# Columns of a matmul taken in pieces: five orders of the moving operand and the PSUM bank in a feed-forward

## The chip, the cores and the metric

The kernel runs on one core of one Trainium2 chip. The metric is the device time of one execution in microseconds (us). Times of whole kernels are medians over runs; the profile comes from one execution of its own.

## The reference

A trunk of two decoder layers over 1024 positions of width 1024, all in float32. Layer 0 mixes by a gated linear recurrence beside attention to a memory of 256 positions; layer 1 mixes by attention in a sliding window of 128 beside memory attention. Each mixer is followed by a gated feed-forward of inner width 2816. The change touches the first half of the feed-forward of layer 0:

```
def swiglu_ffn(x, w_in, w_out):
    gu = x @ w_in
    g, u = gu[..., :D_FF], gu[..., D_FF:]
    return (jax.nn.silu(g) * u) @ w_out
...
f = swiglu_ffn(rms_norm(h, norm_ffn_pre[l]), w_ffn_in[l], w_ffn_out[l])
h = h + rms_norm(f, norm_ffn_post[l])
```

## The kernel before

Activations are kept transposed: 128 features on the partitions, 512 positions along the columns of a tile, so 1024 x 1024 activations are 8 x 2 tiles. To get float32 accuracy from a cheaper matmul format (float32r), each operand is split into a high part, rounded to that format (ScalarE, L95), and the rest (VectorE, L96). A product then takes three matmuls for each 128 features: high weight by low activation (L700), high by high (L701), low by high (L702). All add up in one PSUM bank of 128 x 512 float32. Each matmul reads its 512-column moving operand from SBUF and writes the whole bank; its weights, 128 x 128, are loaded by LDWEIGHTS (in the profile: engine PEld) while the matmul before it still runs.

The inner width of 2816 is 22 blocks of 128. Blocks 0 and 1 are made plainly (`ffn_plain`). Blocks 2 to 21 are made by `gated`: gate and up half of the weights, two halves of the 1024 features and two halves of the positions are treated as 2 x 2 matrices, whose product takes seven block products instead of eight, with sums and differences of weights (GpSimd, L720 to L725) and of activations made beforehand. Each of the seven is one call of `product`: four groups of 128 features, three matmuls each, so 12 matmuls, and 84 for a gated block. The seven add into three banks of tag `mm` (there are seven of them in rotation). `copy`, `gate`, `mul` and `add` read a bank when a product has ended, on ScalarE (L730, L734) and VectorE (L711, L715).

The kernel is written with a framework whose scheduler sets the order of instructions on each engine from priorities (`high_priority`) and its own simulation of time, and which adds the waits between engines. Weights arrive by DMA in the tiles `wq` and `wp`, are split into `ch` and `cl`; activations stand in `ah`/`al` and, for the sums and differences, in `th`/`tl`.

After the blocks, `out_product` (L808 to L810) makes the second half of the feed-forward, and layer 1 follows, with a feed-forward of its own that goes through the same functions with `layer` equal to 1.

Of the kernel before, what the change touches and what calls it, by code (L numbers as in the profile page):

```python
# [43 lines left out]
POST_STEPS = range(4, 20, 2)  # L44
LATE_PRODUCTS, LAST_STEPS = (2, 5, 3), range(36, 132, 12)
OUT_PARTS = {1: (0, 0), 2: (1, 0), 3: (1, 0), 4: (1, 1), 5: (1, 1), 6: (0, 0), 7: (0, 1)}
CLOSE_POOL = (4, "th21"), (5, "tl21")
NO_SYNC = mybir.DependencyInfo(mybir.DependencyClass.NoSync, mybir.DependencyReason.DATA)
SHUF = list(range(8, 16)) + list(range(0, 8)) + list(range(16, 32))
# [2 lines left out]
class Trunk:  # L52
# [639 lines left out]
                hid.append(hu)  # L692
        return hid, mms

    def product(self, out, w, x, start=True):
        mm, ins = self.nc.tensor.matmul, []
        for k in range(4):
            wh, wl = (v[:, k] for v in w)
            xh, xl = x[k]
            ins += [mm(out, wh, xl, start=start and k == 0, stop=False, skip_group_check=not start),  # L700
                    mm(out, wh, xh, start=False, stop=False, skip_group_check=not start),  # L701
                    mm(out, wl, xh, start=False, stop=k == 3, skip_group_check=not start)]  # L702
        return ins

    def gated(self, layer, b, xs, order=(1, 5, 6, 2, 7, 3, 4), ring="wq", eng=None, lead=WEIGHT_LEAD):
        nc = self.nc
        eng = eng or nc.gpsimd
        with self.tc.high_priority(offset=WEIGHT_LEAD):
            a11, a12, a21, a22 = self.quads(ring, *(self.a["wi"][layer, u * NFB + b] for u in range(2)))
        made, sums, hid, part = {}, {}, {}, {}  # L710
        add = lambda o, x, y: nc.vector.tensor_tensor(o, x, y, op=ALU.add)  # L711

        def mul(i, x, y):
            hid[i] = self.t("hd")
            return nc.vector.tensor_tensor(hid[i], x, y, op=ALU.mult)  # L715

        def source(i):
            if i in (5, 6) and 5 not in made:
                made[5] = self.t("x", (P, 4, P))
                eng.tensor_tensor(made[5], a21, a22, op=ALU.add)  # L720
                eng.tensor_tensor(a21, a11, a21, op=ALU.subtract)
            if i == 6:
                eng.tensor_tensor(a11, made[5], a11, op=ALU.subtract)
            if i == 3:
                eng.tensor_tensor(a12, a12, a11, op=ALU.subtract)  # L725
            return {1: a11, 2: a12, 3: a12, 4: a22, 5: made.get(5), 6: a11, 7: a21}[i]

        def copy(i, ps):
            part[i] = self.t({1: "c1", 5: "c7", 6: "c6"}[i])
            return nc.scalar.copy(part[i], ps)  # L730

        def gate(i, ps):
            add(part[i], part[i], ps)
            return nc.scalar.activation(part[i], part[i], AF.Silu)  # L734

        steps = {1: (0, lambda ps: copy(1, ps)),
                 5: (1, lambda ps: copy(5, ps)),
                 6: (0, lambda ps: copy(6, ps)),
                 2: (2, lambda ps: gate(1, ps)),
                 7: (0, lambda ps: add(part[5], part[5], ps)),  # L740
                 3: (1, lambda ps: (gate(6, ps), mul(1, part[6], part[5]))),
                 4: (0, lambda ps: mul(0, part[1], ps))}
        for i in order:
            with self.tc.high_priority(offset=WEIGHT_LEAD if i in (1, 2) else lead):
                src = source(i)
                w = self.t("ch", (P, 4, P), F32R), self.t("cl", (P, 4, P), F32R)
                self.split(*w, src)
            c, evict = steps[i]
            chained = c in sums
            ps = sums.setdefault(c, None if chained else self.psum("mm"))  # L750
            mms = self.product(ps, w, xs[i], start=not chained)
            with self.tc.high_priority(offset=EVICT_LEAD):
                ins = evict(ps)
                if i == 7:
                    self.evicted = ins
            yield mms
        self.hid = hid[0], hid[1]
# [34 lines left out]
    def out_operands(self, layer, i, p, xs, ws):  # L792
        nc = self.nc
        block, half = OUT_PARTS[i]
        src = self.wz[p, block] if i in (3, 5, 6, 7) else self.a["wf"][layer, 2 * p + block]
# [45 lines left out]
    def ffn(self, layer, x, act, hx, finish, dst, final):  # L841
# [133 lines left out]
        for i, cs in enumerate(chunks):  # L975
# [14 lines left out]
            rsc.append(self.rstd([s22[:, cs]] + qs, f"m{i}", "c1", cs.stop - cs.start, copy=i == 0)[1])  # L990
        scaled = {k: self.t(tag)[:, :H // 2] for k, tag in CLOSE_POOL}
        for k, x in scaled.items():
# [402 lines left out]
```

## Time and profile before

| | |
|---|---|
| median of 3 runs | 1966.38 us (1965.18 to 1969.33) |
| profiled execution, whole | 1966.28 us |
| profiled execution, span from first to last instruction | 1964.1 us |
| granted TensorE clock, mean over the span | 0.996 of full speed |
| TensorE matmul (PE), busy | 1937.3 us, 9382 instructions |
| TensorE weight load (PEld), busy | 1629.2 us |
| VectorE (DVE), busy | 1399.5 us |
| ScalarE (ACT), busy | 1017.2 us |
| GpSimd (POOL), busy | 429.1 us |
| DMA, mean | 184 GB/s |

Line numbers are those of the kernel before; in the changed kernel, lines behind the new helper stand five further down (L700 to L702 are L705 to L707). In rows such as `mm<-al,ch 128*128 128x512` the written tile stands before the arrow, then the moving operand and the weights, then the shapes. A busy time of matmuls counts the union of rows that overlap, since one matmul begins before the one ahead of it has left the array.

### The profile page before, as it was taken

The page shows a single profiled execution, that of the slowest core. Times are in us where ns is not written, and L with a number is a line of the kernel's source. Part 1 is how long each engine was busy: PE and PEld are TensorE (multiplying, and loading weights), DVE is VectorE, ACT ScalarE, POOL GpSimd, SP SyncE. Part 2 cuts the span into 40 slices and gives each one's busy share as a digit, 9 for nine tenths or more (in the row PEclk, how much of TensorE's full clock was granted, in tenths as well). Part 3 has the DMA queues.
Part 4 walks back from the last instruction along what each step waited for, and adds up shares of the span by engine and source line. Part 5 has one row for each costly group of instructions (what it writes and reads, how often), then busy time and mean ns, then how long its engine had stood idle before and what let it go on. Part 6 is the DMA issues. An engine that isn't in the chain of part 4 may idle for free.

```text
span 1964.1 us, 27864 instructions
## 1 busy us (share of the span) xinstructions
PE 1937.3 (99%) x9382; PEld 1629.2 (83%) x9382; DVE 1399.5 (71%) x2315; ACT 1017.2 (52%) x1942; POOL 429.1 (22%) x439
## 2 busy tenths in 40 slices
PE   9999999999999999999999999999999999999997
PEld 8887888788888888888788888887888888888887
DVE  8888977976767676455786898669656665754566
ACT  6677974534444444454554778554333333344551
POOL 0122110034443320000035454100223232300001
PEclk9999999999999999999999999999999999999999
DMA  5522436167768789775563333361645444585663
GB/s 185 171 86 81 158 119 227 66 231 256 239 242 279 255 287 326 238 233 174 201 213 141 115 112 108 103 262 39 213 134 168 161 156 153 201 301 194 214 197 129
DMA packets 184686, 361.71 MB, mean 184 GB/s; under 512 B 20448, under 2 KB 26336, under 8 KB 184544
## 3 DMA queue, kind: packets, MB, share of 16 engines
q1 hardware_dynamic: 183824, 359.29, 53.6%
q8 instruction: 73, 1.20, 0.2%
q10 hardware_dynamic: 720, 0.66, 0.1%
q14 instruction: 69, 0.57, 0.1%
HBM read 251.86 MB, written 105.91 MB: 182 GB/s over the span
## 4 chain that ended last, share of the span: by engine, by line
PE 87%; DVE 6%; ACT 3%; issue 2%; DMA 1%; POOL 1%; SPq 0%; DVEq 0%; ACTq 0%; POOLq 0%
PE mm L700 12%; PE mm L702 12%; PE mm L701 12%; PE mm L808 7%; PE mm L809 7%; PE mm L810 7%; PE mm L164 6%; PE mm L165 6%; PE mm L166 6%; PE oo L1210 1%; PE tt L1203 1%; PE mm L680 1%; PE mm L679 1%; PE oo L249 1%; PE mm L681 1%
## 5 line engine op out<-in xcount | busy, mean ns | idle before, releaser
L95 ACT CAST ch<-wq 128x512 fp32r<-128x512 f32 x311 | 193.6, 623 | 419.0 <-PE mm L701 212.1
L96 DVE TENSOR_TENSOR cl<-wq,ch 128x512 fp32r<-128x512 f32 x311 | 237.1, 763 | 186.9 <-ACT ch L95 115.8
L700 PE MATMUL mm<-al,ch 128*128 128x512 f32 x640 | 249.6, 390 | 2.9 <-ACT c L730 2.9
L701 PE MATMUL mm<-ah,ch 128*128 128x512 f32 x640 | 249.2, 389 | 0.0
L702 PE MATMUL mm<-ah,cl 128*128 128x512 f32 x640 | 249.0, 389 | 0.0
L164 PE MATMUL mm<-al,wh 128*128 128x512 f32 x552 | 218.1, 395 | 0.6 <-ACT wh L95 0.6
L165 PE MATMUL mm<-ah,wh 128*128 128x512 f32 x552 | 217.1, 393 | 0.0
L166 PE MATMUL mm<-ah,wl 128*128 128x512 f32 x552 | 216.9, 393 | 0.0
L808 PE MATMUL mm<-tl,ch 128*128 128x512 f32 x532 | 207.4, 390 | 0.6 <-ACT ah L910 0.3
L809 PE MATMUL mm<-th,ch 128*128 128x512 f32 x532 | 207.0, 389 | 0.0
L810 PE MATMUL mm<-th,cl 128*128 128x512 f32 x532 | 206.3, 389 | 0.0
L700 PE MATMUL mm<-tl,ch 128*128 128x512 f32 x480 | 187.4, 390 | 0.2
L701 PE MATMUL mm<-th,ch 128*128 128x512 f32 x480 | 186.8, 389 | 0.0
L702 PE MATMUL mm<-th,cl 128*128 128x512 f32 x480 | 186.6, 389 | 0.2 <-DVE cl L96 0.2
L711 DVE TENSOR_TENSOR c<-c,mm 128x512 f32<-128x512 f32 x120 | 82.4, 686 | 98.6 <-PE mm L702 98.3
L700 PEld LDWEIGHTS mm<-al,ch 128*128 128x128 f32 x640 | 120.2, 188 | 28.3 <-ACT c L730 3.7
L702 PEld LDWEIGHTS mm<-ah,cl 128*128 128x128 f32 x640 | 120.2, 188 | 25.0
L701 PEld LDWEIGHTS mm<-ah,ch 128*128 128x128 f32 x640 | 120.2, 188 | 24.7
L720 POOL TENSOR_TENSOR x<-wq,wq 128x512 f32<-128x512 f32 x36 | 53.8, 1494 | 320.0 <-DMA wq<-in_wi_dram 311.8
L166 PEld LDWEIGHTS mm<-ah,wl 128*128 128x128 f32 x552 | 103.9, 188 | 21.9 <-DVE wl L96 0.7
L164 PEld LDWEIGHTS mm<-al,wh 128*128 128x128 f32 x552 | 103.9, 188 | 21.2 <-ACT wh L95 1.0
L165 PEld LDWEIGHTS mm<-ah,wh 128*128 128x128 f32 x552 | 104.0, 188 | 20.2
(424 smaller groups left out, 4324.8 us busy)
## 6 DMA issues: line engine op xcount, KB each, us to landing
wq<-in_wi_dram SPq DMA_DIRECT2D x168, 256.0 KB, 4.6
xz<-hd SPq DMA_DIRECT2D x154, 256.0 KB, 4.2
th<-xz SPq DMA_DIRECT2D x154, 256.0 KB, 3.5
wp<-in_wf_dram SPq DMA_DIRECT2D x112, 256.0 KB, 4.2
wz<-wp SPq DMA_DIRECT2D x88, 256.0 KB, 2.3
wq<-wz SPq DMA_DIRECT2D x56, 256.0 KB, 3.5
wraw<-in_wa_dram SPq DMA_DIRECT2D x26, 512.0 KB, 3.5
wq<-in_wf_dram SPq DMA_DIRECT2D x42, 256.0 KB, 3.9
```

The source lines that it names most:

```text
L95: self.cast = self.nc.scalar.copy(hi, src)
L96: return (eng or self.nc.vector).tensor_tensor(lo, src, hi.bitcast(F32), op=ALU.subtract)
L164: self.mms += [nc.tensor.matmul(out, wh, al, start=i == 0, stop=False), nc.tensor.matmul(out, wh, ah, start=False, stop=False), nc.tensor. ...
L165: nc.tensor.matmul(out, wh, ah, start=False, stop=False),
L166: nc.tensor.matmul(out, wl, ah, start=False, stop=i == len(ks) - 1)]
L700: ins += [mm(out, wh, xl, start=start and k == 0, stop=False, skip_group_check=not start), mm(out, wh, xh, start=False, stop=False, skip_g ...
L701: mm(out, wh, xh, start=False, stop=False, skip_group_check=not start),
L702: mm(out, wl, xh, start=False, stop=k == 3, skip_group_check=not start)]
L711: add = lambda o, x, y: nc.vector.tensor_tensor(o, x, y, op=ALU.add)
L808: ins += [mm(ps[m], wh[:, m], xl[:, cs], start=start and p == 0, stop=False, skip_group_check=not start), mm(ps[m], wh[:, m], xh[:, cs], s ...
L809: mm(ps[m], wh[:, m], xh[:, cs], start=False, stop=False, skip_group_check=not start),
L810: mm(ps[m], wl[:, m], xh[:, cs], start=False, stop=p == NFB // 2 - 1, skip_group_check=not start)]
```

## The change

`product` gets a further argument `g`, two numbers (b, d). If it is given, the 512 columns are taken as `a` groups of `b` pieces of `d` columns, and the matmul goes through them with the piece number outermost: first piece 0 of every group, then piece 1 of every group, and so on. The PSUM bank and both parts of the moving operand are viewed alike, so each column of the product still lands at its own place in the bank. With (2, 2), for instance, a matmul takes columns 0, 1, 4, 5, 8, 9, ... and then 2, 3, 6, 7, ...; with (2, 128) it takes 0 to 127, 256 to 383, 128 to 255, 384 to 511. Gated blocks from 4 on in layer 0 take their pair from the tuple `WOVEN` by the block's number modulo 6; the first entry is None, so blocks 6, 12 and 18 stay as they were.

```
+WOVEN = None, (2, 2), (2, 8), (2, 16), (8, 16), (2, 128)
...
-    def product(self, out, w, x, start=True):
+    def woven(self, x, g):
+        return x if g is None else x.rearrange("p (a b d) -> p b a d", b=g[0], d=g[1])
+
+    def product(self, out, w, x, start=True, g=None):
         mm, ins = self.nc.tensor.matmul, []
+        out = self.woven(out, g)
         for k in range(4):
             wh, wl = (v[:, k] for v in w)
-            xh, xl = x[k]
+            xh, xl = (self.woven(v, g) for v in x[k])
             ins += [mm(out, wh, xl, start=start and k == 0, stop=False, skip_group_check=not start),
...
-            mms = self.product(ps, w, xs[i], start=not chained)
+            mms = self.product(ps, w, xs[i], not chained, WOVEN[b % 6] if layer == 0 and b > 3 else None)
```

| pattern (b, d) | blocks | pieces in a matmul | shape printed below |
|---|---|---|---|
| none | 6, 12, 18 | 1 | 128x512 |
| (2, 2) | 7, 13, 19 | 256 pieces of 2 | 128x2x128x2 |
| (2, 8) | 8, 14, 20 | 64 pieces of 8 | 128x2x32x8 |
| (2, 16) | 9, 15, 21 | 32 pieces of 16 | 128x2x16x16 |
| (8, 16) | 4, 10, 16 | 32 pieces of 16 | 128x8x4x16 |
| (2, 128) | 5, 11, 17 | 4 pieces of 128 | 128x2x2x128 |

The order of instructions on TensorE, with the semaphores that each waits for, at the place where block 6 ends and block 7 begins (the bank mm_4518 is block 6's, mm_4696 is block 7's first). Before:

```order
L701 MATMUL mm_4518<-th_708_3374,ch_4593 128x512
L702 MATMUL mm_4518<-th_708_3374,cl_4594 128x512
L700 MATMUL mm_4696<-al_3125,ch_4692 128x512 [waits Activation_49]
L701 MATMUL mm_4696<-ah_3124,ch_4692 128x512
L702 MATMUL mm_4696<-ah_3124,cl_4693 128x512 [waits DVE_49]
L700 MATMUL mm_4696<-al_3130,ch_4692 128x512
```

and now:

```order
L706 MATMUL mm_4518<-th_708_3374,ch_4593 128x512
L707 MATMUL mm_4518<-th_708_3374,cl_4594 128x512
L705 MATMUL mm_4696<-al_3125,ch_4692 128x2x128x2 [waits Activation_49]
L706 MATMUL mm_4696<-ah_3124,ch_4692 128x2x128x2
L707 MATMUL mm_4696<-ah_3124,cl_4693 128x2x128x2 [waits DVE_49]
L705 MATMUL mm_4696<-al_3130,ch_4692 128x2x128x2
```

Nothing moved; the shape in which the bank is written is another. So it is at every place of the program: the rows of TensorE differ in 1260 shapes, 252 of each pattern, and those of VectorE, ScalarE, GpSimd and the DMA queue don't differ.

Ten first matmuls of a bank get a wait on TensorE's own count, and one matmul loses such a wait (the first sum over partitions behind the feed-forward). The first of the ten is in block 16, on the same engine. Before:

```order
L701 MATMUL mm_6305<-th_791_3833,ch_6343 128x512
L702 MATMUL mm_6305<-th_791_3833,cl_6344 128x512
L700 MATMUL mm_6365<-al_3145,ch_6361 128x512
L701 MATMUL mm_6365<-ah_3144,ch_6361 128x512
L702 MATMUL mm_6365<-ah_3144,cl_6362 128x512 [waits DVE_49]
```

and now:

```order
L706 MATMUL mm_6305<-th_791_3833,ch_6343 128x8x4x16
L707 MATMUL mm_6305<-th_791_3833,cl_6344 128x8x4x16
L705 MATMUL mm_6365<-al_3145,ch_6361 128x8x4x16 [waits PE_49]
L706 MATMUL mm_6365<-ah_3144,ch_6361 128x8x4x16
L707 MATMUL mm_6365<-ah_3144,cl_6362 128x8x4x16 [waits DVE_49]
```

The matmul that it waits for, the last into the bank before, stands some 180 rows ahead of it; for the nearest of the ten it is some 90 rows.

## The prediction

> **What bounds the kernel now.** I read the page's shares first, then the chain, then the stage that the change touches, and last the single matmuls.
>
> ```profile
> span 1964.1 us, 27864 instructions
> PE 1937.3 (99%) x9382; PEld 1629.2 (83%) x9382; DVE 1399.5 (71%) x2315; ACT 1017.2 (52%) x1942; POOL 429.1 (22%) x439
> PE   9999999999999999999999999999999999999997
> ...
> PE 87%; DVE 6%; ACT 3%; issue 2%; DMA 1%; POOL 1%; SPq 0%; DVEq 0%; ACTq 0%; POOLq 0%
> ```
>
> TensorE is busy for 1937.3 of 1964.1 us, in every slice but the last, and 87% of the chain that ended last is its matmuls. The page also warns that a busy PE need not be PE at its peak, so the stage has to be looked at by itself. The blocks that the change touches run from about 406.5 to 756.0 us. The columns of the next rows are the stretch, its length, busy time with number of instructions of PE, PEld, DVE, ACT and POOL, the granted clock, the DMA share and GB/s.
>
> ```profile
> 406.50:756.00 349.50, 349.31 (x1541) 288.93 (x1540) 251.79 (x346) 150.05 (x262) 134.28 (x94) 1.00 0.76 263
> 478.32:497.36 19.04, 19.04 (x85) 15.77 (x85) 11.19 (x16) 7.92 (x14) 8.87 (x6) 1.00 0.68 232
> ...
> 744.88:763.92 19.04, 19.04 (x85) 15.77 (x85) 12.06 (x20) 9.62 (x17) 0.00 (x0) 1.00 0.95 327
> ```
>
> TensorE is idle for 0.2 of 349.5 us, at a granted clock of 1.00, while VectorE and ScalarE have a quarter to a half of each block free. One block is 7 products of 12 matmuls, 84 in all, and takes 19.04 us, so a matmul takes 19.04/84 = 226.7 ns from start to start. The single rows agree:
>
> ```profile
> 468.41 0.39 PE L700 MATMUL mm<-tl,ch 128*128 128x512 f32 x1
> 468.63 0.39 PE L701 MATMUL mm<-th,ch 128*128 128x512 f32 x1
> 468.86 0.39 PE L702 MATMUL mm<-th,cl 128*128 128x512 f32 x1
> 469.09 0.39 PE L700 MATMUL mm<-tl,ch 128*128 128x512 f32 x1
> ```
>
> Each lasts 0.39 us but the next starts 0.227 us after it: they overlap. The price of a matmul is the 226.7 ns between starts, not the 0.39 us of its row. Whatever a matmul of this stage gains or loses in start-to-start time goes straight to the end of the kernel, because nothing else sets the pace here, nor afterwards:
>
> ```profile
> PE mm L702 <- DVE cl L96: 0.2, 1, 0.2
> ...
> 756.00:1000.00 244.00, 242.90 (x1102) 201.31 (x1102) 148.97 (x244) 120.78 (x220) 10.24 (x9) 1.00 0.65 219
> 1000.00:1300.00 300.00, 295.14 (x1759) 260.00 (x1758) 238.46 (x552) 195.84 (x509) 113.70 (x162) 0.99 0.44 155
> 1300.00:1660.00 360.00, 357.85 (x1595) 295.52 (x1594) 242.89 (x350) 141.70 (x241) 87.75 (x61) 1.00 0.43 146
> 1660.00:1930.00 270.00, 270.00 (x1255) 226.21 (x1254) 167.20 (x253) 127.17 (x226) 24.12 (x17) 1.00 0.62 207
> ```
>
> The first row is the only wait of TensorE in 406 to 756 us (us in total, times, longest). The others show 1.1, 4.9, 2.2 and 0.0 us of idle TensorE in the four later stretches: there is no later slack in which a loss could vanish.
>
> **The change, part by part.** It adds no instruction and removes none; the order on VectorE, ScalarE, GpSimd and the DMA queue is the same row for row. What changes is the order in which 15 of the 18 blocks take the 512 columns: 15 x 84 = 1260 matmuls, 252 in each of the five patterns (blocks 6, 12 and 18 stay plain). Moving operand and PSUM bank are permuted alike, so the same columns meet and the readers of the bank find them where they were. LDWEIGHTS reads the same 128 contiguous columns as before.
>
> The term that decides is 1260 times the difference in start-to-start time of a plain and a woven matmul. No plain matmul of this kernel reads its moving operand or writes its bank in pieces, so the trace has no row for it, and I bound it from both sides.
>
> From below: what a matmul spends beyond its columns. Ten matmuls of 256 columns stand between these first two rows, and the third has eight of 128 columns in another format:
>
> ```profile
> 996.69 0.28 PE L1257 MATMUL mm<-wh,al 128*128 128x256 f32 x1
> ...
> 997.88 1.05 PE L261 MATMUL oo<-ident,rcp 128*128 128x128 f32 x8
> ...
> L261 PE MATMUL oo<-ident,rcp x56: 270/275/275, 284.1 to 1905.5; 128*128 128x128 f32 x56
> ```
>
> (997.88 - 996.69)/10 = 119.0 ns for 256 columns. So a column costs (226.7 - 119.0)/256 = 0.421 ns, and a matmul has 226.7 - 512 x 0.421 = 11.3 ns besides its columns. A new order of the columns can't make fewer of them; if it saved all of the 11.3 ns, 1260 matmuls would give 14.2 us, the end below. That part is alike at 256 and at 512 columns, so it belongs to the instruction and not to the order, and I expect nothing of it.
>
> From above: the slowest columns that the trace has. The eight of L261 are plain fp32, not the split format of the products; (1.05 - 0.275)/7 = 110.7 ns for 128 columns, against 0.06 us here for a matmul of 128 columns in the split format:
>
> ```profile
> 1080.16 0.22 PE L1179 MATMUL ss<-kl,qs 128*128 128x128 f32 x1
> 1080.22 0.28 PE L1180 MATMUL ss<-kh,qs 128*128 128x128 f32 x1
> ```
>
> Columns at about half the rate therefore exist on this engine: 4 x 110.7 = 443 ns for 512, 216 ns over the plain price. If all five patterns ran so, 1260 x 216 ns = 272 us; if only one did, 252 x 216 ns = 54.5 us.
>
> Between the ends I take the value of the rows nearest to "in pieces", although they are of ScalarE and of LDWEIGHTS. L377 writes its 256 columns as four runs of 64 with gaps of 64, L359 the same 256 without gaps; L261's weights are one column read 128 times, L700's lie side by side (the source view: ns min/median/max):
>
> ```profile
> L359 ACT ACTIVATE gi<-mm,rcm 128x256 f32<-128x256 f32 x4 | 1.9, 473 | 4.2 <-POOL rcm L254 4.1
> L377 ACT ACTIVATE vv<-mm,rcn 128x256 fp32r<-128x256 f32 x4 | 1.9, 473 | 3.5 <-PE mm L1259 3.5
> ...
> L261 PEld LDWEIGHTS oo<-ident,rcp x56: 187/190/192, 283.9 to 1905.4; 128*128 128x128 f32 x56
> L700 PEld LDWEIGHTS mm<-al,ch x640: 186/188/192, 328.9 to 1739.5; 128*128 128x128 f32 x160
> ```
>
> 473 against 473 ns, and 190 against 188: a pattern with steps costs nothing there. Both are slower per column than a matmul (473/256 = 1.8 ns against 0.421), so they say little of the finest pieces, and that is where I leave room.
>
> [...]
>
> Beside the patterns, the new program makes ten first matmuls of a bank wait on TensorE's own count, and drops one such wait. In the order the bank's former matmuls lie a block or more back, 19 us, so the wait is over when it is reached: 0. If each instead let the matmul before it drain, it would cost 389 - 227 = 162 ns, ten of them 1.6 us (389 is the median of the row below, min/median/max).
>
> ```profile
> L700 PE MATMUL mm<-al,ch x640: 389/389/499, 328.9 to 1739.7; 128*128 128x512 f32 x160
> ```
>
> Sum: 0 + 0. The profiled execution took 1966.28 us (span 1964.1), 0.1 below the median of the three runs; I give the median, 1966.4.
>
> **Rivals.**
> 1. *Pieces of two columns are too fine.* In pattern (2, 2) a pass takes two columns and skips two, so wherever the operand's memory or the bank serves four neighbours or more at once, half of what is fetched or opened is left for the second pass. It decides as soon as that service is the slower side. Then the 252 matmuls of blocks 7, 13 and 19 run at half rate: 54.5 us by the row above, 252 x 226.7 ns = 57.1 us if the whole matmul doubles. That gives 2020.8 to 2023.4. For it: a block has no idle microsecond to hide it. Against it: pieces of 8 and more, four of the five patterns, would be served whole, and nothing in the trace shows such a limit.
>    [...]
> 2. *Each break costs a column's time.* Pieces per matmul are 256, 64, 32, 32 and 4, together 388; 388 x 0.421 ns x 252 = 41.2 us, 2007.5. For it: a break needs a new address. Against it: three gaps on L377 cost under 1 ns together.
> 3. *All five patterns run at half rate*, because any step in the pattern makes the bank open each column by itself: 1966.3 + 272 = 2239. Against it: pieces of 128 columns have three breaks in 512. [...]
> 4. *Faster*, by the 11.3 ns of a matmul, down to 1952. Only if that gap came from neighbouring columns meeting in the bank; its being alike at two sizes speaks against it.
>
> **How the numbers follow.** A change of 0.2%, 3.9 us, is about what a measurement of this kernel can tell from none; it is 3.1 ns on each woven matmul, or 15.6 ns if only (2, 2) pays. No cost: 0.57. Rival one 0.27, two 0.06, three 0.07, faster 0.03. So slower 0.27 + 0.06 + 0.07 = 0.40, same 0.57, faster 0.03. The likeliest case alone would lie in 1962 to 1971 (0.2% either way, with the 1.6 us of the waits). With rival one the range has to reach 2024, and then holds 0.57 + 0.27 + 0.06 = 0.90; left out are rival three and a gain.
>
> **What would show it.** In the profile after, 406 to 756 us should keep blocks of 19.04 us, with L705 to L707 at 389 ns in every shape. Rival one shows as blocks of some 37 us from about 463, 578 and 692 us on (later ones shifted by what was lost), at busy TensorE and otherwise unchanged waits; rival two as blocks of graded length, rival three as 15 long blocks with three short ones among them. A loss with all blocks at 19.04 us would mean that I missed a wait. The prediction is wrong, too, if the clock in the stage falls below 1.00.

## The result, and the profile after

The changed kernel takes 2029.1 us (median of 4 runs, 2027.18 to 2030.15) where the kernel before takes 1966.1 (4 runs on the same chip, 1965.18 to 1969.33): a ratio of 1.0316, with a 95% interval of 1.0298 to 1.0334. It is slower by 63 us, in the direction and nearly by the amount of rival one, and above the top of the range.

The page of the changed kernel, its span and busy row, then the shares of the chain that ended last:

```profile
span 2027.8 us, 27863 instructions
PE 1999.1 (99%) x9382; PEld 1632.8 (81%) x9382; DVE 1396.3 (69%) x2315; ACT 1017.4 (50%) x1942; POOL 425.7 (21%) x439
PE 88%; DVE 6%; ACT 2%; issue 2%; DMA 1%; POOL 0%; SPq 0%; DVEq 0%; ACTq 0%; POOLq 0%
```

TensorE is busy for 61.8 us more with the same 9382 matmuls; the other engines are busy as long as they were, to within 4 us. Nothing else became the bound. The stretches of the first half of the feed-forward, from its first gated matmul to the first matmul of the second half (L700 to L808 before, L705 to L813 now), before and after (stretch, length, busy time with instructions of PE, PEld, DVE, ACT and POOL, clock, DMA share, GB/s):

```profile
328.95:756.05 427.10, 424.77 (x1885) 350.36 (x1884) 313.82 (x447) 184.74 (x320) 139.31 (x98) 1.00 0.66 227
```

```profile
330.25:820.72 490.47, 487.92 (x1884) 355.58 (x1884) 311.10 (x447) 185.96 (x320) 137.21 (x98) 1.00 0.58 200
```

The stage is 63.4 us longer, TensorE's idle time in it is 2.3 us before and 2.6 after, and the clock stays at 1.00. So the whole loss is matmuls that take longer, in this stage, and the span (+63.7) shows that nothing of it was won back later. The single matmuls say which ones. First where block 7, pattern (2, 2), begins behind a plain bank, then inside it, then inside block 9, pattern (2, 16) (start, duration):

```profile
471.99 0.39 PE L706 MATMUL mm<-th,ch 128*128 128x512 f32 x1
472.22 0.39 PE L707 MATMUL mm<-th,cl 128*128 128x512 f32 x1
472.45 0.61 PE L705 MATMUL mm<-al,ch 128*128 128x512 f32 x1
...
479.68 0.64 PE L706 MATMUL mm<-th,ch 128*128 128x512 f32 x1
480.13 0.63 PE L707 MATMUL mm<-th,cl 128*128 128x512 f32 x1
480.59 0.63 PE L705 MATMUL mm<-tl,ch 128*128 128x512 f32 x1
...
532.86 0.40 PE L705 MATMUL mm<-tl,ch 128*128 128x512 f32 x1
533.09 0.41 PE L706 MATMUL mm<-th,ch 128*128 128x512 f32 x1
533.34 0.40 PE L707 MATMUL mm<-th,cl 128*128 128x512 f32 x1
```

A (2, 2) matmul starts 0.45 us after the one ahead of it; its own duration rises from 0.39 to 0.63 us. A (2, 16) matmul shows almost nothing in its duration, 0.40, but its neighbours start 0.23 and 0.25 us apart. Again the start-to-start time is the price. Its mean over the 84 matmuls of a block, from all single rows of the stage, is the same to 0.2 ns in the three blocks of each pattern (neighbouring blocks interleave by some products, so a block's matmuls are counted by their banks). For (2, 2) the table has the price in an unbroken row inside the block; the mean of all 84 is 452.3 ns, which makes 56.9 us. The plain 226.7 ns are those of the kernel before; the plain blocks 12 and 18 stand at 227.2 here.

| pattern | pieces | ns from start to start | more than plain, ns | x 252 matmuls, us |
|---|---|---|---|---|
| none | 1 | 226.7 | | |
| (2, 2) | 256 of 2 | 453.3 in an unbroken row | 226.6 | 57.1 |
| (2, 8) | 64 of 8 | 232.9 | 6.2 | 1.6 |
| (2, 16) | 32 of 16 | 239.8 | 13.1 | 3.3 |
| (8, 16) | 32 of 16 | 231.7 | 5.0 | 1.3 |
| (2, 128) | 4 of 128 | 227.4 | 0.7 | 0.2 |

The sum is 63.5 us, or 63.3 with the mean of all 84, against 63.4 measured in the stage. Pattern (2, 2) takes twice the plain time and makes 90% of the loss. The last column is not in the order of the number of pieces.

### The profile page after: what moved, and what is told of

It reads as the page before. It is cut to its first block, busy times and chain, and to the rows that moved or that the text cites. A ratio compares the mean times of both kernels' runs of the same rounds, so it can differ in the third digit from the quotient of the medians.

```text
span 2027.8 us, 27863 instructions
## 1 busy us (share of the span) xinstructions
PE 1999.1 (99%) x9382; PEld 1632.8 (81%) x9382; DVE 1396.3 (69%) x2315; ACT 1017.4 (50%) x1942; POOL 425.7 (21%) x439
## 4 chain that ended last, share of the span: by engine, by line
PE 88%; DVE 6%; ACT 2%; issue 2%; DMA 1%; POOL 0%; SPq 0%; DVEq 0%; ACTq 0%; POOLq 0%
PE mm L705 13%; PE mm L707 13%; PE mm L706 13%; PE mm L813 7%; PE mm L814 7%; PE mm L815 7%; PE mm L165 6%; PE mm L167 6%; PE mm L166 6%; PE oo L1215 1%; PE oo L250 1%; PE tt L1208 1%; PE mm L681 1%; PE mm L680 1%; PE mm L682 1%
## 5 line engine op out<-in xcount | busy, mean ns | idle before, releaser
L97 DVE TENSOR_TENSOR cl<-wq,ch 128x512 fp32r<-128x512 f32 x311 | 232.4, 748 | 232.3 <-ACT ch L96 124.0
L705 PE MATMUL mm<-al,ch 128*128 128x512 f32 x640 | 262.4, 410 | 2.8 <-ACT c L735 2.8
L706 PE MATMUL mm<-ah,ch 128*128 128x512 f32 x640 | 262.0, 409 | 0.0
L707 PE MATMUL mm<-ah,cl 128*128 128x512 f32 x640 | 262.0, 409 | 0.0
L813 PE MATMUL mm<-tl,ch 128*128 128x512 f32 x532 | 207.4, 390 | 0.6 <-ACT ah L915 0.3
L814 PE MATMUL mm<-th,ch 128*128 128x512 f32 x532 | 207.0, 389 | 0.0
L815 PE MATMUL mm<-th,cl 128*128 128x512 f32 x532 | 206.4, 389 | 0.0
L705 PE MATMUL mm<-tl,ch 128*128 128x512 f32 x480 | 196.9, 410 | 0.2
L707 PE MATMUL mm<-th,cl 128*128 128x512 f32 x480 | 196.2, 409 | 0.4 <-DVE cl L97 0.4
L706 PE MATMUL mm<-th,ch 128*128 128x512 f32 x480 | 196.4, 409 | 0.0
L705 PEld LDWEIGHTS mm<-al,ch 128*128 128x128 f32 x640 | 121.2, 189 | 39.6 <-issue 11.8
```

The source lines that it names most:

```text
L97: return (eng or self.nc.vector).tensor_tensor(lo, src, hi.bitcast(F32), op=ALU.subtract)
L813: ins += [mm(ps[m], wh[:, m], xl[:, cs], start=start and p == 0, stop=False, skip_group_check=not start), mm(ps[m], wh[:, m], xh[:, cs], s ...
L814: mm(ps[m], wh[:, m], xh[:, cs], start=False, stop=False, skip_group_check=not start),
L815: mm(ps[m], wl[:, m], xh[:, cs], start=False, stop=p == NFB // 2 - 1, skip_group_check=not start)]
```

## The experiments

Theories after the result: S, the cost lies in reading the moving operand from SBUF; P, it lies in writing the PSUM bank; B, both pay, one for (2, 2) and the other for the rest; and for the size, several that follow. Line numbers in the rows are those of each kernel; L704 to L711 are always the three matmuls of `product`.

**Which side pays.** The first kernel weaves the moving operand alone:

```
-        out = self.woven(out, g)
```

> Only the moving operand is taken in pieces; the PSUM bank is written in order, so in 15 blocks the columns of the product land in other places than the reference's. The changed kernel showed per matmul, start to start: 226.7 ns plain, 453 in (2, 2), 232.7 in (2, 8), 239.8 in (2, 16), 231.4 in (8, 16), 227.4 in (2, 128). Theory S, the read of SBUF pays for the pieces: all five numbers stay, and the kernel takes about 2029 us. Theory P, the write into the PSUM bank pays: all five fall to 226.7 ns and the kernel takes about 1966 us. Theory B, both pay, one for (2, 2) and the other for the rest: 2023 us with the doubling here, or 1972 us without it.

Measured: 2030.7 us (one run), span 2027.5. Inside the first (2, 2) block:

```profile
480.05 0.63 PE L705 MATMUL mm<-th,ch 128*128 128x512 f32 x1
480.50 0.64 PE L706 MATMUL mm<-th,cl 128*128 128x512 f32 x1
480.95 0.63 PE L704 MATMUL mm<-tl,ch 128*128 128x512 f32 x1
```

The second weaves the bank alone:

```
-            xh, xl = (self.woven(v, g) for v in x[k])
+            xh, xl = x[k]
```

> The counterpart: the moving operand is read in order and only the PSUM bank is written in pieces, again with columns in other places than the reference's in 15 blocks. Theory S (read of SBUF pays): 226.7 ns in every block, 1966 us. Theory P (write into the bank pays): the five numbers of the changed kernel, 2029 us. Theory B: 1972 or 2023 us, whichever moving-only does not show.

Measured: 1966.3 us (one run), span 1964.1, the same as before. Its page, the stage, one block's time, and matmuls that write the bank by (2, 2), in this order:

```profile
span 1964.1 us, 27863 instructions
```

```profile
406.50:756.00 349.50, 349.50 (x1542) 289.00 (x1541) 256.80 (x347) 149.75 (x263) 133.62 (x94) 1.00 0.76 264
470.00:489.04 19.04, 19.04 (x85) 15.77 (x85) 13.05 (x18) 6.77 (x12) 7.87 (x5) 1.00 0.79 274
```

```profile
472.31 0.39 PE L707 MATMUL mm<-ah,cl 128*128 128x512 f32 x1
472.54 0.39 PE L705 MATMUL mm<-tl,ch 128*128 128x512 f32 x1
472.77 0.39 PE L706 MATMUL mm<-th,ch 128*128 128x512 f32 x1
473.00 0.39 PE L707 MATMUL mm<-th,cl 128*128 128x512 f32 x1
```

S holds; P and B fall. With the operand alone every pattern has its price of the changed kernel to within 1 ns; with the bank alone every block, of whatever pattern, stays at 226.7 ns, but for block 6, in which TensorE is held up once in the kernel before as well (a mean of 232.9 ns there, 230.4 here). This kernel carries the ten added waits too and takes 1966.3 us, so they cost nothing, as the prediction had it. Even 256 pieces of two columns cost the bank nothing that can be measured: 19.04 us for the 84 matmuls of a block, as before. Single columns were not tried.

**Is it (2, 2) alone?** The third kernel makes blocks 7, 13 and 19 plain:

```
-WOVEN = None, (2, 2), (2, 8), (2, 16), (8, 16), (2, 128)
+WOVEN = None, None, (2, 8), (2, 16), (8, 16), (2, 128)
```

> As the changed kernel, but blocks 7, 13 and 19 are plain; the four coarser patterns stay. By start-to-start times (theory T) the doubling is 252 x 226.7 ns = 57.1 us and the other four patterns are 252 x (6.2 + 13.1 + 5.0 + 0.7 ns) = 6.3 us: 1972.5 us, 0.3% over the kernel before, with 232.7, 239.8, 231.4 and 227.4 ns unchanged. Rival W, the rest beyond the doubling is a wait or a shift that only the slow blocks bring: 1966 us.

Measured: 1972.1 us (7 runs, 1971.29 to 1974.42) against 1966.1 (10 runs): a ratio of 1.0034 (1.0022 to 1.0045). Theory T holds: even pieces of 8 to 128 cost 6 us together, a small loss, but every one of the 7 runs lies above all 10 of the kernel before (1963.93 to 1967.85).

**How does the price go with the size of a piece?** The fourth kernel has five other patterns:

```
+WOVEN = None, (4, 2), (2, 4), (4, 4), (2, 32), (128, 2)
```

> Both sides in pieces as in the changed kernel, with other patterns: (4, 2), (2, 4), (4, 4), (2, 32), (128, 2) in place of the five. Theory U, memory serves four neighbouring columns at a time, and each visit to such a group costs the time of four columns at half use: (4, 2) 453 ns, (128, 2) 453, (2, 4) and (4, 4) near 227 to 240, (2, 32) between 227 and 240; 2 x 57 us + some 6 = about 2087 us. Theory H, memory is halved by pairs of columns, and a pair that follows one of the same half waits: (4, 2) 453 or more, (2, 4) and (4, 4) near 227 as their pairs alternate, but (128, 2) about 340, as only every other step stays in its half: about 2057 us. Theory N, a break costs by its number: (2, 4) with 128 pieces and (4, 4) with 128 alike, and between (2, 2) and (2, 8), about 300 ns or more: over 2110 us.

Measured: 2056.4 us (one run). (4, 2) 460.7 ns, (2, 4) 233.7, (4, 4) 224.0, (2, 32) 236.5, (128, 2) 339.6. This is what theory H said, in the whole time and in each pattern that it priced; U is 113 ns too high for (128, 2), and N falls with (2, 4) and (4, 4), which it put near 300 ns. That H is wrong all the same takes the next two kernels to see. Pieces of four are enough, and (4, 4) is 2.7 ns faster than plain.

The fifth gives each block from 4 to 21 a pattern of its own:

```
+WOVEN = ((4, 4), (8, 4), (16, 4), (32, 4), (64, 4), (4, 8),
+         (8, 8), (16, 8), (32, 8), (64, 8), (4, 16), (16, 16),
+         (4, 32), (8, 32), (2, 64), (64, 2), (32, 2), (8, 2))
...
+            mms = self.product(ps, w, xs[i], not chained, WOVEN[b - 4] if layer == 0 and b > 3 else None)
```

> Both sides in pieces, one pattern for each of the 18 blocks: (4, 4), (8, 4), (16, 4), (32, 4), (64, 4), (4, 8), (8, 8), (16, 8), (32, 8), (64, 8), (4, 16), (16, 16), (4, 32), (8, 32), (2, 64), (64, 2), (32, 2), (8, 2). (64, 8) is the plain order. Theory H (SBUF hands out pairs of columns from two halves in turn, even pairs and odd pairs, and a pair that follows one of its own half takes twice the time): with (64, 2) four pairs of one half follow each other, so 3 of 4 wait, 1.75 x 226.7 = 397 ns; (32, 2) 7 of 8, 425 ns; (8, 2) all, 453 to 461 ns; all patterns with pieces of 4 and more, whose pairs alternate, between 224 and 240 ns. Theory U (four neighbours are fetched at a time and nothing is kept): 453 ns in all three with pieces of 2. Theory K (the last two fetches of four are kept): (64, 2) and (32, 2) 453 ns, since more than two places are visited in turn. The kernel takes about 2016 us by H and 2023 us by U and K. No theory here says why (4, 4) came out at 224.0 ns, under the plain 226.7; if that is a property of stride, (8, 4) and (16, 4) show it too.

Measured: 2040.6 us (one run), above every theory. Pieces of two: (64, 2) 443.8 ns, (32, 2) 487.0, (8, 2) 431.3. Pieces of four: 224.2, 246.3, 276.4, 267.6 and 250.7, in the order of the tuple. Pieces of eight: 224.5, 256.8, 231.2, 243.0, 227.6; of 16: 238.9, 240.0; of 32: 233.6, 236.5; of 64: 227.4. H is off by 47 and 62 ns for (64, 2) and (32, 2); the 453 ns of U and K is nearer for (64, 2), but (32, 2) lies well above it. There is a step between two and four columns, and above it a spread from 224 to 276 ns that follows neither the number of pieces nor their length and that no theory had.

**What makes the step?** The sixth kernel uses the first n of the 512 columns, so that the number of pieces can be odd and a piece can have 6, 10 or 14 columns; the first matmul into each bank, 3 of 84 in a block, takes all columns plainly:

```
+WOVEN = ((1, 2, 512), (1, 2, 504), (3, 2, 510), (5, 2, 510), (7, 2, 504), (6, 2, 504),
+         (3, 4, 504), (5, 4, 500), (7, 4, 504), (2, 6, 504), (3, 6, 504), (2, 10, 500),
+         (3, 8, 504), (7, 8, 504), (3, 16, 480), (5, 16, 480), (3, 32, 480), (2, 14, 504))
...
+        return x if g is None else x[:, :g[2]].rearrange("p (a b d) -> p b a d", b=g[0], d=g[1])
```

> One pattern for each block, with group lengths that are not powers of two, so the last 2 to 32 columns of a bank are left out of all but the first matmul of a bank (the product is incomplete there). Columns used: (b, d, n) = plain 512, plain 504, (3, 2, 510), (5, 2, 510), (7, 2, 504), (6, 2, 504), (3, 4, 504), (5, 4, 500), (7, 4, 504), (2, 6, 504), (3, 6, 504), (2, 10, 500), (3, 8, 504), (7, 8, 504), (3, 16, 480), (5, 16, 480), (3, 32, 480), (2, 14, 504). Theory H (two halves, even and odd pairs): an odd step lets pieces of 2 alternate, so (3, 2), (5, 2) and (7, 2) run near the plain price, 220 to 240 ns, while (6, 2) takes about 450; (2, 6) has a clash every third pair, 4/3 x 224 = 298 ns; (3, 6) none, 220 to 240; (2, 10) one in five, 1.2 x 222 = 266; (2, 14) one in seven, 1.14 x 224 = 255. Theory U (fetches of four neighbours, each visit costs): (3, 2), (5, 2), (7, 2) like (6, 2), about 450 ns, and (2, 6) and (3, 6) alike. Kernel: about 2000 us by H, above 2050 us by U.

Measured: 2054.0 us (one run). Theory H, that even and odd pairs lie in different halves of something, falls: odd counts cost as much as even ones. The other, U, says that the moving operand comes in aligned groups of four neighbouring fp32 columns (16 bytes), and that each visit to such a group costs four columns' time. Pieces of six columns decide best, since they visit 8/6 = 1.33 times as many columns as they use. Rows of block 13, pattern (2, 6):

```profile
669.69 0.47 PE L708 MATMUL mm<-tl,ch 128*128 128x504 f32 x1
669.99 0.47 PE L710 MATMUL mm<-th,ch 128*128 128x504 f32 x1
670.29 0.47 PE L711 MATMUL mm<-th,cl 128*128 128x504 f32 x1
```

They start 0.30 us apart; the woven matmuls of the block, with the three plain ones taken out, come to 300.0 ns, and 504 columns at the plain price (226.7 - 8 x 0.421 = 223.3 ns) by 1.33 are 297.8. Likewise (3, 6) 300.0, which H put at 220 to 240; (2, 10), 12/10, 273.6 against 266.0; (2, 14), 16/14, 253.4 against 255.2; pieces of two 434 to 454 against 447 to 452. The plain 504 columns of this kernel were measured at 227.2 ns and not at 223.3, so U's figures are good to some 2%. And pieces of whole groups spread here too: (5, 4), of 500 columns, takes some 256 ns.

**Is it where a piece begins, or how long it is?** The seventh kernel weaves the operand alone and begins its window at column 0 or at column 2, so that a piece of four covers one aligned group or half of two:

```
+        return x if g is None else x[:, g[3]:g[3] + g[2]].rearrange("p (a b d) -> p b a d", b=g[0], d=g[1])
```

> Only the moving operand is in pieces, a different pattern for each of the blocks 4 to 21, with the window of columns begun at column 0 or at column 2 (some columns are left out or land in another place of the bank, so the output isn't the reference's; 3 matmuls of 84 in a block stay plain). Theory U (the operand comes in aligned groups of four columns, 16 bytes, and each visit to a group costs four columns' time): pieces of 4 begun at column 2 straddle two groups and double, (1, 4) excepted, since its pieces follow each other: (3, 4) and (2, 4) 226 to 234 ns at 0, some 447 at 2; (3, 8) at 2 visits 3 groups for 8 columns, 340 ns; (3, 12) at 2 300 ns; (3, 24) at 2 265 ns; (1, 4) 227 at either. (2, 2) is 447 at either. Theory L (what counts is the length of a piece, wherever it begins): no difference between 0 and 2. For (126, 2), (84, 2), (63, 4) and (126, 4), where a piece is followed by only one, two or no other before its neighbour comes: if a group that was fetched is kept for a while, (126, 2) is near 340 ns as (128, 2) was, and (84, 2) lies between it and 447.

Measured: 2093.6 us (one run). Rows of blocks 7 and 6, the same pattern (3, 4) of 504 columns, begun at column 2 and then at column 0:

```profile
473.51 0.62 PE L708 MATMUL mm<-al,ch 128*128 128x504 f32 x1
473.95 0.62 PE L710 MATMUL mm<-ah,ch 128*128 128x504 f32 x1
474.40 0.62 PE L711 MATMUL mm<-ah,cl 128*128 128x504 f32 x1
...
480.71 0.39 PE L711 MATMUL mm<-ah,cl 128*128 128x504 f32 x1
480.93 0.38 PE L708 MATMUL mm<-al,ch 128*128 128x504 f32 x1
481.15 0.39 PE L710 MATMUL mm<-ah,ch 128*128 128x504 f32 x1
```

| pattern | begun at 0, ns | begun at 2, ns | U at 2, ns |
|---|---|---|---|
| (1, 4), in a row | 227.1 | 229.4 | 225 |
| (3, 4) | 224.9 | 446.5 | 447 |
| (2, 4) | 228.0 | 446.1 | 447 |
| (3, 8) | 236.5 | 330.4 | 335 |
| (3, 12) | | 300.6 | 298 |
| (3, 24) | | 267.9 | 261 |
| (2, 2) | 449.4 | 447.2 | 447 |

(Three plain matmuls of 84 are taken out; U is 223.3 ns times the groups visited over the groups covered.) Two columns of offset, 8 bytes, about double the time of (3, 4), from 224.9 to 446.5 ns, and of (2, 4), from 228.0 to 446.1, though not of (1, 4), whose pieces follow each other (227.1 and 229.4): L falls, and U holds for what a visit to part of a group costs. Whether the limit sits in SBUF itself or in the path that reads it, and whether the unit is four columns or 16 bytes, no run here separates. U leaves two things unexplained. One is the spread: (16, 4) takes 276.4 ns on whole groups, and (32, 2) 487.0 where U has 453. The other is a group that is left for only one or two other visits and then visited again, which costs less than twice: (128, 2) in the fourth kernel 339.6 ns, here (126, 2) 325 and 334, one other visit between; (84, 2) 370, two between; with three between, (64, 2), it is 443.8. (63, 4) begun at 2, with one other piece between, takes 327 and not 447. No run here shows why.

**Is a faster order to be had?** The fourth and the fifth kernel had (4, 4) at 224.0 and 224.2 ns, below plain. The eighth has it on both sides in all gated blocks of both layers, the ninth also in the projections, the plain blocks and the second half of the feed-forward:

```
+WOVEN = 4, 4
...
+            mms = self.product(ps, w, xs[i], not chained, WOVEN)
```

> Pattern (4, 4) on both sides, in every gated block of both layers: 40 blocks of 84 matmuls = 3360. In the two runs that had blocks of (4, 4), a matmul took 224.0 and 224.2 ns from start to start against 226.5 to 226.9 plain. Theory F (that gain is a property of the pattern and holds wherever TensorE is the bound): 3360 x 2.6 ns = 8.7 us less, some 1957.5 us, all 20 blocks of layer 0 at 18.8 us. Theory G (it came from the neighbouring blocks or from the weight load's luck in those runs): blocks stay at 226.5 to 227 ns, 1966 us.

> Pattern (4, 4) in the gated blocks and also in the projections, in the plain blocks and in the second half of the feed-forward (some 7300 matmuls of 512 columns or, some, of 256). Theory F: 7300 x 2.6 ns = 19 us less where TensorE is the bound throughout, 1947 us; some of it may be lost where TensorE already waits (0.2 to 5 us idle in each stretch), so 1947 to 1952. Theory G: 1966 us.

Measured: 1965.5 us (12 runs) against 1966.35 (17 runs), a ratio of 0.9992 (0.9983 to 1.0), and 1959.7 us (6 runs, 1953.96 to 1961.79), a ratio of 0.9960 (0.9947 to 0.9974). The eighth is no faster than the kernel before beyond the noise; the ninth is, by 6.7 us and not by 19. Groups of the projections, before and in the ninth kernel (busy us, mean ns of one):

```profile
L164 PE MATMUL mm<-al,wh 128*128 128x512 f32 x552 | 218.1, 395 | 0.6 <-ACT wh L95 0.6
```

```profile
L165 PE MATMUL mm<-al,wh 128*128 128x512 f32 x552 | 215.6, 391 | 0.8 <-ACT wh L96 0.8
```

Shorter rows alone prove nothing: those of the gated blocks shrink as well, from 390 and 389 to 388 and 387 ns, and nothing is gained there. The starts decide. The first matmuls of blocks 7 and 21, before and in the ninth kernel:

```profile
470.45 0.39 PE L700 MATMUL mm<-al,ch 128*128 128x512 f32 x1
...
737.01 0.39 PE L700 MATMUL mm<-al,ch 128*128 128x512 f32 x1
```

```profile
468.48 0.39 PE L705 MATMUL mm<-al,ch 128*128 128x512 f32 x1
...
735.04 0.39 PE L705 MATMUL mm<-al,ch 128*128 128x512 f32 x1
```

Two us are gained ahead of block 7 and none from there to block 21. By the starts of the same matmuls in the two profiles the rest comes between some 925 and 1460 us (2.9 us) and behind 1886 us (1.5), so mostly in the stages where TensorE pauses now and then. In the long rows of gated blocks, in the eighth and the ninth kernel, the blocks 7 to 21 are at 226.3 to 226.8 ns, 19.04 us each as before, though not evenly: of every eight matmuls most start 0.22 or 0.23 us after the one ahead, and two that follow each other take 234 and 239 ns. So neither theory holds as it stood: the gain is real, but a long row of (4, 4) can lose it.

Two more kernels asked why. The tenth puts other patterns between blocks of (4, 4):

```
+F, S = (4, 4), (8, 8)
+WOVEN = F, F, F, S, F, F, F, F, F, None, F, None, F, (2, 16), F, F, F, F
```

> Why did (4, 4) take 224 ns from start to start in single blocks and 226.7 ns when all blocks had it? Here the blocks 4, 5, 6 have (4, 4), 7 has (8, 8) (256.8 ns), 8 to 12 (4, 4), 13 plain, 14 (4, 4), 15 plain, 16 (4, 4), 17 (2, 16) (239.8 ns), 18 to 21 (4, 4), on both sides. Theory C (a limit on the sustained rate, 226.7 ns a matmul, against which slower work before builds up credit): the (4, 4) blocks right behind the slow blocks 7 and 17 at 224.0 ns and later ones back at 226.7 when the credit is spent; 14 and 16, behind plain blocks, at 226.7. Theory N (a (4, 4) block is slowed by a (4, 4) block ahead of it): 4, 8, 14, 16 and 18 at 224.0, those behind them at 226.7. Theory R (it differs from program to program): all alike.

Measured: 1964.4 us (one run). Blocks 4 and 5 at 223.8 ns; 8 at 227.9 and 9 to 12 at 226.7; 14 and 16, behind plain blocks, at 224.2 and 224.0; 18 to 21, in a row, at 223.3 to 223.8. The blocks 11 and 19, both (4, 4) among their like:

```profile
546.06:565.10 19.04, 19.04 (x86) 15.77 (x84) 12.54 (x18) 8.17 (x14) 6.37 (x6) 1.00 0.77 263
698.97:717.73 18.76, 18.76 (x85) 15.74 (x84) 12.99 (x19) 8.53 (x15) 4.16 (x3) 1.00 0.87 295
```

All three theories fail: a row of four blocks holds 223.3 ns, a row of five holds 226.7, in one program. Each unbroken row of (4, 4) seen here keeps one of two paces; the slow one repeats every eight matmuls, the fast one every four. (8, 8) has more than one pace as well, and changes it inside a block: in block 7 its first 23 matmuls take 253 ns in the mean, and later 40 in a row hold 233.3. Over the block it took 240.6 ns, against 256.8 in the fifth kernel.

The eleventh takes only 448 of the columns, plainly in blocks 4 to 12, by (4, 4) in 13 to 21:

```
+WOVEN = ((1, 4, 448, 0),) * 9 + ((4, 4, 448, 0),) * 9
```

> What is it that is limited to 226.7 ns? In the blocks 4 to 21 all matmuls but the first into each bank (81 of 84) take only 448 columns of the moving operand, plainly in blocks 4 to 12 and by (4, 4) in 13 to 21; the last 64 columns are left out. Theory I (a limit on matmuls, each with its load of weights, per time): 226.7 ns stays, and the kernel keeps its 1966 us. Theory K (a limit on columns per time, or none for plain matmuls): 226.7 - 64 x 0.421 = 199.7 ns, with the three plain ones 200.7 in the mean, 18 x 84 x 26 ns = 39 us less, 1927 us, unless TensorE then waits for weights. In 13 to 21 it tells whether (4, 4) saves its 2.6 ns in a long row when there are fewer columns: 198 ns if so, 200.7 if not.

Measured: 1946.1 us (one run; 1966.85 before). Within block 12, and then TensorE's waits and the stretch of these blocks:

```profile
567.74 0.37 PE L706 MATMUL mm<-al,ch 128*128 128x448 f32 x1
567.95 0.37 PE L708 MATMUL mm<-ah,ch 128*128 128x448 f32 x1
568.15 0.37 PE L709 MATMUL mm<-ah,cl 128*128 128x448 f32 x1
```

```profile
PE mm L709 <- DVE cl L97: 5.7, 10, 1.0
PE mm L706 <- ACT ch L96: 2.1, 6, 1.3
```

```profile
413.20:735.50 322.30, 313.24 (x1513) 280.48 (x1511) 250.00 (x339) 143.95 (x259) 133.63 (x92) 1.00 0.80 277
```

No limit of 226.7 ns per matmul exists (theory I falls): in the plain blocks without a wait, 4, 6 and 12, a matmul takes 205.4 to 207.3 ns in the mean. That is above the 200.7 that the price of a column gave, and the (4, 4) blocks without a wait, 16 and 19, are at 198.4 and 196.8. Half of the 39 us expected doesn't arrive: TensorE is now idle for 9 us, most of it waiting for weights to be split, and the rest goes into matmuls that start later than 200.7 ns apart. What sets the two paces stays open.

## Why the prediction was wrong

- **What bounds the kernel**: right. The stage had no idle time to take up a loss, and none of the loss came back later: 63.4 us in the stage, 63.7 in the span, 63.0 in the medians.
- **The term that decides, 1260 matmuls at 0**: wrong, and this is the step that failed: they cost 63.4 us, some 57 of it in the 252 matmuls of (2, 2). I took the value of the rows "nearest to in pieces", of ScalarE and of LDWEIGHTS, at zero, with 0.57 of the chance. Those rows move a column in 1.8 and 1.5 ns; a matmul takes 0.421. By U a visit to a group takes the time of four columns, 4 x 0.421 = 1.7 ns (an estimate), about what those rows spend on one column, so they could hardly have shown the price; no run tests them with finer pieces. I said that they "say little of the finest pieces" and still let them decide. They were also the wrong kind of step: L377 steps in what it writes, where the price is in a read, and its runs of 64 columns hold whole groups of four, and such runs cost the moving operand next to nothing as well ((2, 64) 227.4 ns).
- **Rival one**: right in its mechanism, its blocks and its size, 57.1 us for 252 matmuls at double time (measured 57.1 by the unbroken row and 56.9 by the mean of all; the other bound, 54.5 from the fp32 matmuls of L261, was some 2.5 too low). It named "the operand's memory or the bank"; it is the reading of the operand alone, by the first two kernels (0.45 us from start to start with the operand in pairs, 226.7 ns with the bank), and a unit of four columns fits what the sixth and the seventh show ((2, 6) 300.0 ns where U has 297.8, (3, 4) 224.9 on the group and 446.5 off it). The blocks that were to be "some 37 us from about 463, 578 and 692" are 84 x 452.3 ns = 38.0 us from 472, 608 and 743; the starts were some 7 us early already for the kernel before, where block 7 begins at 470.45. Its chance of 0.27 was too low.
- **Pieces of 8 and more "would be served whole"**: nearly. They cost 6.3 us, which no case had beside the 57.1; the third kernel shows them alone, at 6.0 us. The range ended at 2024 because rival one stood there without them; with them it is 1966.4 + 63.4 = 2029.8, against 2029.1 measured.
- **Rival two, a column's time at each break**: wrong. 64 breaks of (2, 8) cost 6.2 ns and 32 of (2, 16) cost 13.1, where a column's time each would make 26.9 and 13.5. (2, 16) comes near by chance: (8, 16) has as many breaks and costs 5.0. Pieces that hold whole groups have prices that go with the stride, from 223.3 ns for (4, 4) to 276.4 for (16, 4), in a way I can't give a rule for.
- **Rival three, the bank**: wrong; in the second kernel the bank is free in all five patterns, at 226.7 ns a matmul, and no run shows it open columns one by one.
- **The ten waits**: right, 0; they stand in the second kernel, which has the time of before (1966.3 us).
- **Faster, "alike at two sizes, so it belongs to the instruction"**: not forecast to happen and it did not in this change, but the reason was wrong. (4, 4) saves 2.5 to 3.4 of the 11.3 ns, so they are not all fixed. Nor was it an observation that the part is alike at two sizes: a line through two points makes it so, and the third size, 448 columns in the eleventh kernel, lies some 5 ns off that line.

## What to carry to other kernels

Where TensorE ran matmul behind matmul here, the order in which its fp32 moving operand was read was a cost: 453.3 ns by pairs against 226.7 plain. Keep each run of columns in whole, aligned groups of four (16 bytes; (3, 4) took 224.9 ns on the group, 446.5 off it), and count the groups that a pattern visits, not its pieces ((2, 6), with 8/6 visits, took 300.0 ns). Whole groups are not free at every stride: 512 columns took from 223.3 to 276.4 ns here, so measure the pattern that you mean to use. On the PSUM side the five orders of the change, down to pieces of two, cost nothing (226.7 ns). Where a profile shows no row for the operation in question, rows of slower work are no evidence that it is free: here rows at 1.8 and 1.5 ns a column showed no price for their steps, and matmuls at 0.421 ns a column took twice their time by pairs.

## What the runs showed of the hardware

- A matmul of 512 fp32 columns (in the split format) whose operand is read by pairs, pattern (2, 2), takes 453.3 ns from start to start in an unbroken row instead of 226.7, while the same order on the bank takes 226.7.
- Pieces of four columns begun two columns off the group, pattern (3, 4), take 446.5 ns for a matmul of 504 columns, on the group 224.9.
- Read by pairs, with the second half of a group after one other visit, pattern (128, 2), a matmul takes 339.6 ns, 1.5 times the plain 226.7; after two others, (84, 2) of 504 columns, 370, 1.66 times the 223.3 worked out for them; after three, (64, 2), 443.8, 1.96 times 226.7.
- (4, 4) runs at 223.3 to 224.2 ns or at 226.7, a whole row of blocks alike, in the same program. In the slow rows two of every eight matmuls take 234 and 239 ns, and plain matmuls, with all 84 intervals at 226 or 227 ns, have just the mean of the slow pace. No run here shows why.
